# Low products eight places behind the high ones in the feed-forward stages of a two-layer hybrid block

## The chip, the cores and the metric

The kernel runs on one core of one Trainium2 chip. The metric is device time in microseconds (us). The kernel before takes 2301.96 us, the median of 3 runs (2301.77 to 2302.32).

## What is computed

Two layers, each a mixer (four kinds of attention, left out here) and a gated feed-forward part, on 256 positions of width 2048, in float32. The change touches only the up projection of the feed-forward part:

```python
def reference(x, norm_mix_pre, ...):
    ...
    for l in range(DEPTH):
        ...
        hin = _rms_norm(x, norm_mlp_pre[l])
        u = hin @ mlp_w_up[l]                    # 256x2048 @ 2048x11264
        u_pad = jnp.pad(u, ((0, 0), (CONV_WIDTH - 1, 0), (0, 0)))
        conv = mlp_conv_b[l] + mlp_conv_w[l][0] * u_pad[:, 0:s_len]
        for tap in range(1, CONV_WIDTH):
            conv = conv + mlp_conv_w[l][tap] * u_pad[:, tap:tap + s_len]
        gate, up = jnp.split(conv, 2, axis=-1)
        y = (jax.nn.gelu(gate, approximate=True) * up) @ mlp_w_down[l]
        x = x + _rms_norm(y, norm_mlp_post[l])
```

## The kernel before

**Split numbers.** TensorE takes a rounded float32 format here (float32r), so each float32 operand is used as a sum of a high and a low part. The activations lie in four tiles `HL0` to `HL3`, each 128 x 4 x 512: for each of the 16 slices `k` of the contraction, 256 columns of high parts and 256 of low parts. A weight tile is split on the chip: ScalarE (ACT) copies the loaded tile `raw` into `hi` (line 192), VectorE (DVE) subtracts to get `lo` (line 195). A **high product** multiplies a 128 x 128 piece of `hi` with all 512 columns of a slice; a **low product** multiplies the matching piece of `lo` with the 256 high columns alone. Both add into one PSUM bank.

**Units and granules.** One unit is 128 output columns of the up projection: 16 slices, so 16 high and 16 low products into one bank. Its weights come as two granules of 128 x 1024 (eight slices each). In each feed-forward stage 88 units run. The first three go through `start_block`, which also moves the activations into `HL0` to `HL3`; the other 85 are issued by `w_unit` (line 635), one unit after another. Then `out_units` (line 693) does the down projection with products of 512 columns.

**Order of the products.** `mm_runs` (line 426) issues the eight high products of a unit's first granule, then its eight low ones; for the second granule the low ones, then the high ones. Along the stage that makes runs of 16 low products (two half runs of one unit) and of 16 high products (the end of one unit and the start of the next):

```python
        for f in (los, his) if h else (his, los):
            f()
```

`start_block` uses `mm_w` (line 417) for its last pieces, in which low and high products alternate (lines 421 and 422).

**What sets the order elsewhere.** The program order of every engine is fixed when the program is built. `run_gran` (line 282) goes through one granule: `fill("v")` lets every waiting chain of small work take one step, `ready` (line 215) issues the loads and splits up to `LOOK` = 5 granules ahead, then come the products, `used` marks the granule's tiles as free for later ones (six `hi` and six `lo` tiles go round, line 204: the split of a granule may be issued only after the granule six before it was marked), and `fill("pe")`. When a unit's second granule is done, `launch` puts its evacuation among the chains (lines 1476 to 1506): ScalarE copies one half of the bank to `u`, VectorE adds the other, scales by the row norm `r2bc`, runs the three-tap convolution, and gate and up are joined in `y`. The scale `r2bc` is made near the start of each stage by the chain `rows` (line 488): GpSimd writes `diag`, one TensorE product (line 498) spreads it over the partitions, and ScalarE copies the result (line 500). There are eight PSUM banks, and `room` (line 279) advances chains until one is free.

Of the kernel before, what the change touches and what calls it, by code (L numbers as in the profile page):

```python
# [22 lines left out]
KT = D // 128  # L23
FF = 5632
NF = FF // 128
# [12 lines left out]
SPLIT_US = 1.15  # L38
# [97 lines left out]
def hybrid_kernel(ctx, tc, a):  # L136
    nc = tc.nc
    V, SC, TE, GP = nc.vector, nc.scalar, nc.tensor, nc.gpsimd
# [3 lines left out]
    ps = ctx.enter_context(tc.tile_pool(name="ps", bufs=1, space=bass.MemoryType.PSUM))  # L142
# [6 lines left out]
    def take(kind):  # L149
        live[kind] += 1  # L150
        assert live[kind] <= cap[kind], kind

    def drop(kind, n=1):
        live[kind] -= n
        assert live[kind] >= 0, kind

    def bank():
        take("ps")
        return ps.tile([128, 512], F32, tag="ps", name="bank", bufs=8)
# [4 lines left out]
    def gran(src, c0, n, whole=False):  # L164
        return Granule(src[:, c0:c0 + n], n, whole)

    def add(f, *gs):
        work.append((f, gs))
# [32 lines left out]
    def prep(upto, how=split):  # L201
        while state["gran"] <= min(upto, len(grans) - 1):
            i = state["gran"]
            if i >= HL_BUFS and grans[i - HL_BUFS].uses > 0:
                return
            g = grans[i]
            load(i + RAW_BUFS - 1)
            if state["load"] <= i:
                return
            if not g.whole:  # L210
                g.hi, g.lo = split_tiles()
                how(g, 0, g.n)
            state["gran"] += 1

    def ready(g, look=LOOK):
        prep(g.idx + look)
        assert g.idx < state["gran"]

    def used(g):
        g.uses -= 1  # L220
# [5 lines left out]
    def launch(gen, cost=0.0):  # L226
        c = Chain(gen)
        budget[0] -= cost
        if c.kind is not None:
            active.append(c)  # L230
        return c

    def may(c):
        return (all(live[k] + n <= lim[k] for k, n in c.need.items())
                and (c.cond is None or c.cond()))

    def step(c):
        c.step()
        if c.kind is None:
            active.remove(c)  # L240

    def fill(kind):
        n = 0
        for c in list(active):
            if c.kind == kind and may(c):
                step(c)
                n += 1
        return n

    def start(gain):  # L250
        budget[0] = min(budget[0] + gain, 2.0)
        n = 0
        while budget[0] > 0:
            for i in range(min(3, len(queue))):
                cost, fn, cond = queue[i]
                if cond is None or cond():
                    c = Chain(fn())
                    if not may(c):
                        continue
                    del queue[i]  # L260
                    budget[0] -= cost
                    active.append(c)
                    if c.kind == "pe":
                        step(c)
                    n += 1
                    break
            else:
                break
        return n
# [4 lines left out]
    def force(cond):  # L274
        while not cond():
            n = fill("v") + fill("pe") + start(1.0)
            assert n or budget[0] <= 0, "no chain can go on"

    def room(kind, n=1):
        force(lambda: live[kind] + n <= cap[kind])  # L280

    def run_gran(g, us, emit):
        fill("v")
        ready(g)
        emit()
        used(g)
        fill("pe")
        start(us - SPLIT_US)
# [25 lines left out]
    HL = [None] * 4  # L314
# [52 lines left out]
    def hview(k):  # L367
        return HL[k // 4][:, k % 4, :256]
# [57 lines left out]
    def mm_runs(o, g, h):  # L426
        def his():
            for k in range(8 * h, 8 * h + 8):
                TE.matmul(o, lhsT=g.hi[:, k % 8 * 128:k % 8 * 128 + 128], rhs=HL[k // 4][:, k % 4, :],  # L429
                          start=(k == 0), stop=(k == KT - 1))  # L430

        def los():
            for k in range(8 * h, 8 * h + 8):
                TE.matmul(o[:, :256], lhsT=g.lo[:, k % 8 * 128:k % 8 * 128 + 128], rhs=hview(k),  # L434
                          start=False, stop=False)

        for f in (los, his) if h else (his, los):
            f()
# [196 lines left out]
    def w_unit(src, evac, cost):  # L635
        u = src
        gs = [gran(u, 0, 1024), gran(u, 1024, 1024)]
        box = {}

        def part(h):  # L640
            def run():
                def emit():
                    if h == 0:
                        room("ps")
                        box["a"] = bank()
                    mm_runs(box["a"], gs[h], h)
                run_gran(gs[h], 2.56, emit)
                if h == 1:
                    launch(evac(box["a"]), cost)
            return run  # L650
        add(part(0), gs[0])
        add(part(1), gs[1])

    def x_units(srcs, width, evac, cost):
        box = {}
# [196 lines left out]
    def over():  # L852
        while ends:
            ends.pop()()
# [15 lines left out]
    def mixer(l):  # L870
# [542 lines left out]
        for h in range(4):  # L1413
            main.append(lambda h=h: w_unit(W[l, h], evac_nsa_q(h), 1.9))
# [45 lines left out]
    def mlp(l):  # L1460
        st = {}

        def begin():
            over()
            es = ExitStack()
            mp = es.enter_context(tc.tile_pool(name=f"mlp{l}", bufs=1, reuse_waits="tile"))
            st["es"], st["mp"], st["done"] = es, mp, set()
            st["cw"] = mp.tile([128, 2 * NF + 8, 4], F32, name="cw")[:, :2 * NF]
            GP.dma_start(out=st["cw"], in_=a["conv"][l])
            st["y"] = [mp.tile([128, 256], F32, name=f"y{j}") for j in range(NF)]  # L1470
            on_rows[0] = lambda: None

        def evac(i):
            j, up = divmod(i, 2)

            def f(p, first=None):
                yield "v", dict(u=1)
                mp = st["mp"]
                take("u")
                u = mp.tile([128, 256], F32, tag="u", name="u", bufs=4)  # L1480
                SC.activation(u, p[:, 256:], AF.Copy)  # L1481
                yield "v"
                V.tensor_tensor(u, u, p[:, :256], op=OP.add)  # L1483
                drop("ps")
                if first is not None:
                    add_first(u, first)
                if not scaled[0]:
                    yield "v", {}, is_scaled
                V.tensor_tensor(u, u, r2bc, op=OP.mult)  # L1489
                cv = mp.tile([128, 256], F32, tag="cv", name="cv", bufs=5)  # L1490
                w = st["cw"][:, i]
                V.tensor_scalar(cv, u, w[:, 2:3], w[:, 3:4], op0=OP.mult, op1=OP.add)  # L1492
                for tap in (1, 0):
                    n = 2 - tap
                    V.scalar_tensor_tensor(cv[:, n:], u[:, :256 - n], w[:, tap:tap + 1], cv[:, n:], op0=OP.mult,  # L1495
                                           op1=OP.add)
                drop("u")
                if not up:
                    yield "v"
                    g = mp.tile([128, 256], F32, tag="gl", name="gl", bufs=3)  # L1500
                    SC.activation(g, cv, AF.Gelu_apprx_tanh)  # L1501
                    st["g", j] = g
                else:
                    yield "v", {}, lambda: ("g", j) in st
                    V.tensor_tensor(st["y"][j], st["g", j], cv, op=OP.mult)
                    st["done"].add(j)
            return f

        UP = a["w_up"]
        start_block(2 * l + 1, [UP[l, i] for i in range(3)], [evac(i) for i in range(3)], mgs)  # L1510
        add(begin)
        for i in range(3, 2 * NF):
            w_unit(UP[l, i], evac(i), 0.0)
        out_units(2 * l + 1, lambda p_, k2: a["w_down"][l, p_, k2], NF, lambda k: st["y"][k],
                  lambda k: k in st["done"], mgs, tail_norm(mgs) if l < DEPTH - 1 else tail_out(mgs),
                  Left(lambda: st["mp"].tile([128, 256], F32R, tag="xs", name="xs", bufs=12), "xs"),
                  lambda: st["mp"].tile([128, 1024], F32, tag="gpost", name="gpost"), l == DEPTH - 1)

        def end():
            live["xs"] = 0  # L1520
            st["es"].close()
        add(lambda: ends.append(end))
# [3 lines left out]
    for l in range(DEPTH):  # L1526
        mixer(l)
        mlp(l)
# [95 lines left out]
```

## Time and profile before

| what | value |
|---|---|
| median of 3 runs | 2301.96 us |
| the profiled execution's own time | 2302.25 us |
| its span, from first to last instruction | 2300.5 us |
| mean granted TensorE clock | 0.999 of full speed |
| TensorE products (PE) | 2284.5 us busy, 99% of the span |
| weight loads (PEld) | 1971.7 us, 86% |
| VectorE | 1682.6 us, 73% |
| ScalarE | 1173.2 us, 51% |
| GpSimd | 50.0 us, 2% |
| DMA | 437.56 MB, mean 190 GB/s |

Busy times of products overlap, since an instruction's record runs from its start to a modelled end, while the next has started. So what one product costs is read here from start to start, in the timeline view: a row there gives the start in us, the time from the first start to the last end, engine, line, operation and tiles, the count of merged instructions, and in brackets the idle time before them and what ended it. A run of n products lasts from its row's start to the next row's start.

### The profile page before, as it was taken

What the parts mean: (1) busy time and instruction counts of PE and PEld (TensorE: products, weight loads), DVE (VectorE), ACT (ScalarE), POOL (GpSimd) and SP (SyncE); (2) the same over time, 40 slices, a digit from 0 to 9 for tenths busy, and PEclk for the clock granted to TensorE, in tenths of its full rate; (3) what the DMA queues carried; (4) which work ended last, traced back from release to release, by engine and by line L of the source; (5) the groups of instructions that cost most, each with busy time, mean ns of one, the idle gap of its engine ahead of it and who ended that gap; (6) DMA issues with size and microseconds to landing.
All of it is one profiled execution on the core that took longest, in us unless ns stands there. A gap on an engine that the chain in (4) does not pass through costs nothing.

```text
span 2300.5 us, 33209 instructions
## 1 busy us (share of the span) xinstructions
PE 2284.5 (99%) x12476; PEld 1971.7 (86%) x12476; DVE 1682.6 (73%) x2888; ACT 1173.2 (51%) x1915; POOL 50.0 (2%) x71
## 2 busy tenths in 40 slices
PE   8999999999999999999999999999999999999998
PEld 7888888888888888888888888888888888888887
DVE  6757656898888888565586576568988888885655
ACT  6454555644444444555464555556444444445543
POOL 1000000100000000000010000001000000000000
PEclk9999999999999999999999999999999999999999
DMA  8764455466556555656557645554665555556663
GB/s 277 249 218 150 159 167 199 156 207 199 192 184 192 190 187 184 202 187 211 176 189 239 209 141 174 174 193 158 207 197 188 191 190 185 191 191 194 202 194 116
DMA packets 122658, 437.56 MB, mean 190 GB/s; under 512 B 13888, under 2 KB 14016, under 8 KB 122496
## 3 DMA queue, kind: packets, MB, share of 16 engines
q1 hardware_dynamic: 120384, 429.40, 57.0%
q0 software_dynamic: 1824, 5.94, 0.9%
q8 instruction: 98, 1.61, 0.3%
q14 instruction: 64, 0.52, 0.1%
q10 hardware_dynamic: 288, 0.10, 0.0%
HBM read 433.28 MB, written 2.10 MB: 189 GB/s over the span
## 4 chain that ended last, share of the span: by engine, by line
PE 96%; ACT 1%; DVE 1%; issue 1%; DMA 0%; POOL 0%; SPq 0%; DVEq 0%; POOLq 0%; ACTq 0%
PE bank L429 36%; PE bank L434 19%; PE bank L728 9%; PE bank L726 9%; PE bank L727 9%; PE bank L678 2%; PE bank L680 2%; PE bank L679 2%; PE bank L1146 1%; PE bank L1068 1%; ACT hi L192 1%; PE bank L422 1%; PE bank L466 0%; PE bank L381 0%; DVE x L410 0%
## 5 line engine op out<-in xcount | busy, mean ns | idle before, releaser
L195 DVE TENSOR_TENSOR lo<-raw,hi 128x1024 fp32r<-128x1024 f32 (+1 forms) x786 | 948.3, 1211 | 499.1 <-ACT hi L192 498.3
L192 ACT ACTIVATE hi<-raw 128x1024 fp32r<-128x1024 f32 (+1 forms) x786 | 815.7, 1046 | 435.4 <-PE bank L728 265.5
L429 PE MATMUL bank<-HL,hi 128*128 128x512 f32 x3648 | 880.5, 392 | 0.4 <-DVE u L1483 0.4
L429 PEld LDWEIGHTS bank<-HL,hi 128*128 128x128 f32 x3648 | 669.3, 188 | 130.9 <-issue 2.8
L434 PEld LDWEIGHTS bank<-HL,lo 128*128 128x128 f32 x3648 | 469.5, 191 | 21.5 <-DVE qk L943 1.6
L434 PE MATMUL bank<-HL,lo 128*128 128x256 f32 x3648 | 480.3, 284 | 0.0
L726 PE MATMUL bank<-hi,xs 128*128 128x512 f32 x960 | 374.7, 390 | 0.0
L728 PE MATMUL bank<-hi,xs 128*128 128x512 f32 x960 | 373.9, 390 | 0.0
L727 PE MATMUL bank<-lo,xs 128*128 128x512 f32 x960 | 373.8, 389 | 0.0
L728 PEld LDWEIGHTS bank<-hi,xs 128*128 128x128 f32 x960 | 180.3, 188 | 37.4
L727 PEld LDWEIGHTS bank<-lo,xs 128*128 128x128 f32 x960 | 180.3, 188 | 37.3
L726 PEld LDWEIGHTS bank<-hi,xs 128*128 128x128 f32 x960 | 180.3, 188 | 36.7
L1495 DVE SCALAR_TENSOR_TENSOR cv<-u,cw,cv 128x255 f32<-128x255 f32 x352 | 170.1, 483 | 12.5
L1481 ACT ACTIVATE u<-bank 128x256 f32<-128x256 f32 x176 | 66.7, 381 | 202.2 <-PE bank L429 202.2
L1501 ACT ACTIVATE gl<-cv 128x256 f32<-128x256 f32 x88 | 36.8, 418 | 222.2 <-DVE cv L1495 222.2
L678 PE MATMUL bank<-hi,HL 128*128 128x512 f32 (+1 forms) x256 | 97.6, 381 | 0.5 <-ACT r2bc L500 0.5
L680 PE MATMUL bank<-hi,HL 128*128 128x512 f32 (+1 forms) x256 | 93.6, 366 | 0.0
L679 PE MATMUL bank<-lo,HL 128*128 128x512 f32 (+1 forms) x256 | 93.5, 365 | 0.0
L1489 DVE TENSOR_TENSOR u<-u,r2bc 128x256 f32<-128x256 f32 x176 | 74.9, 426 | 5.8
L1492 DVE TENSOR_SCALAR cv<-u,cw 128x256 f32<-128x256 f32 x176 | 72.7, 413 | 6.4
L1483 DVE TENSOR_TENSOR u<-u,bank 128x256 f32<-128x256 f32 x176 | 72.9, 414 | 0.0
L699 DVE TENSOR_TENSOR xs<-y,xs 128x256 fp32r<-128x256 f32 x176 | 72.2, 418 | 0.0
(212 smaller groups left out, 1388.5 us busy)
## 6 DMA issues: line engine op xcount, KB each, us to landing
raw<-in_w_up SPq DMA_DIRECT2D x352, 512.0 KB, 4.3
raw<-in_w_down SPq DMA_DIRECT2D x176, 512.0 KB, 3.7
raw<-in_w_cols SPq DMA_DIRECT2D x122, 512.0 KB, 4.2
raw<-in_w_out SPq DMA_DIRECT2D x64, 512.0 KB, 4.4
raw<-in_w_v SPq DMA_DIRECT2D x48, 512.0 KB, 4.3
raw<-in_cmp SPq DMA_DIRECT2D x32, 512.0 KB, 4.6
gpost<-in_gpost POOLq DMA_DIRECT2D x8, 512.0 KB, 7.2
raw<-in_w_x SPq DMA_DIRECT2D x8, 408.0 KB, 4.0
```

The source lines that it names most:

```text
L192: SC.activation(g.hi[:, c0:c0 + n], g.raw[:, c0:c0 + n], AF.Copy)
L195: eng.tensor_tensor(g.lo[:, c0:c0 + n], g.raw[:, c0:c0 + n], g.hi[:, c0:c0 + n].bitcast(F32), op=OP.subtract)
L429: TE.matmul(o, lhsT=g.hi[:, k % 8 * 128:k % 8 * 128 + 128], rhs=HL[k // 4][:, k % 4, :], start=(k == 0), stop=(k == KT - 1))
L434: TE.matmul(o[:, :256], lhsT=g.lo[:, k % 8 * 128:k % 8 * 128 + 128], rhs=hview(k), start=False, stop=False)
L678: TE.matmul(o, lhsT=h, rhs=wh, start=(K == 0), stop=False)
L679: TE.matmul(o, lhsT=h, rhs=wl, start=False, stop=False)
L680: TE.matmul(o, lhsT=lo, rhs=wh, start=False, stop=(K == KT - 1))
L726: TE.matmul(o, lhsT=h_, rhs=wh, start=(k[1] == 0), stop=False)
L727: TE.matmul(o, lhsT=h_, rhs=wl, start=False, stop=False)
L728: TE.matmul(o, lhsT=l_, rhs=wh, start=False, stop=(k[1] == nk - 1))
L1489: V.tensor_tensor(u, u, r2bc, op=OP.mult)
L1495: V.scalar_tensor_tensor(cv[:, n:], u[:, :256 - n], w[:, tap:tap + 1], cv[:, n:], op0=OP.mult, op1=OP.add)
```

## The change

`w_unit` is replaced, for the 85 later units of both feed-forward stages, by `w_lagged`. A granule's eight high products are issued at its own turn; its eight low products are issued in the next granule's turn, one ahead of each high product there. So the products alternate low, high, low, high from the second granule of the stage to the last, and a last step `flush` issues the eight low products that are left. The granule is marked as used, and a unit's evacuation launched, one granule later than before.

```diff
+    def w_lagged(units):
+        back = []
+
+        def lo(j):
+            g, h, o, _ = back[0]
+            k = 8 * h + j
+            TE.matmul(o[:, :256], lhsT=g.lo[:, j * 128:(j + 1) * 128], rhs=hview(k), start=False, stop=(k == KT - 1))
+
+        def done():
+            g, h, o, evac = back.pop()
+            used(g)
+            if h:
+                launch(evac(o))
+
+        def part(g, h, box, evac):
+            def run():
+                fill("v")
+                ready(g)
+                if h == 0:
+                    room("ps")
+                    box.append(bank())
+                for j in range(8):
+                    k = 8 * h + j
+                    if back:
+                        lo(j)
+                    TE.matmul(box[0], lhsT=g.hi[:, j * 128:(j + 1) * 128], rhs=HL[k // 4][:, k % 4, :],
+                              start=(k == 0), stop=False)
+                if back:
+                    done()
+                back.append((g, h, box[0], evac))
+                fill("pe")
+                start(2.56 - SPLIT_US)
+            return run
...
+        def flush():
+            for j in range(8):
+                lo(j)
+            done()
+        add(flush)
...
-        for i in range(3, 2 * NF):
-            w_unit(UP[l, i], evac(i), 0.0)
+        w_lagged([(UP[l, i], evac(i)) for i in range(3, 2 * NF)])
```

**TensorE, one unit in the middle of the first feed-forward stage.** The rows give line, operation, the bank written, the activation tile, the weight tile (`hi_4378` and `lo_4379` are the first granule, `hi_4384` and `lo_4385` the second), the moving columns, waits and count. Before:

```order
L429 MATMUL bank_4521<-HL0_4021,hi_4378 128x512 x3
L429 MATMUL bank_4521<-HL1_4022,hi_4378 128x512 x4
L434 MATMUL bank_4521<-HL0_4021,lo_4379 128x256 x4
L434 MATMUL bank_4521<-HL1_4022,lo_4379 128x256 x4
L434 MATMUL bank_4521<-HL2_4023,lo_4385 128x256 x4
L434 MATMUL bank_4521<-HL3_4024,lo_4385 128x256 x4
L429 MATMUL bank_4521<-HL2_4023,hi_4384 128x512 x4
L429 MATMUL bank_4521<-HL3_4024,hi_4384 128x512 x4
```

The same unit (now in `bank_4504`; line 679 is the high product, line 660 the low one) with the change, at the turn of its second granule:

```order
L660 MATMUL bank_4504<-HL0_4021,lo_4379 128x256
L679 MATMUL bank_4504<-HL2_4023,hi_4384 128x512
L660 MATMUL bank_4504<-HL0_4021,lo_4379 128x256
L679 MATMUL bank_4504<-HL2_4023,hi_4384 128x512
L660 MATMUL bank_4504<-HL0_4021,lo_4379 128x256
L679 MATMUL bank_4504<-HL2_4023,hi_4384 128x512
```

The runs of 16 are gone: each low product of the first granule stands ahead of a high product of the second.

**TensorE, the spreading product of line 498 near the start of the first feed-forward stage.** `bank_4388` is the first of the 85 units, `bank_4447` before and `bank_4431` now the second. Before:

```order
L434 MATMUL bank_4388<-HL3_4024,lo_4257 128x256 x4
L429 MATMUL bank_4388<-HL2_4023,hi_4256 128x512 [waits Activation_49]
L429 MATMUL bank_4388<-HL2_4023,hi_4256 128x512 x3
L429 MATMUL bank_4388<-HL3_4024,hi_4256 128x512 x4
L498 MATMUL bank_4436<-diag_73,cst_66 128x256 [waits PE_49,Pool_49]
L429 MATMUL bank_4447<-HL0_4021,hi_4262 128x512 [waits DVE_49,PE_49,Activation_49]
```

Now:

```order
L679 MATMUL bank_4388<-HL3_4024,hi_4256 128x512
L498 MATMUL bank_4422<-diag_73,cst_66 128x256 [waits PE_49,Pool_49]
L660 MATMUL bank_4388<-HL2_4023,lo_4257 128x256 [waits DVE_49]
L679 MATMUL bank_4431<-HL0_4021,hi_4262 128x512 [waits Activation_49]
L660 MATMUL bank_4388<-HL2_4023,lo_4257 128x256
L679 MATMUL bank_4431<-HL0_4021,hi_4262 128x512
```

Line 498 moved ahead by eight low products, one low product follows it, and the first high product of the next bank waits for ScalarE alone where it waited for VectorE too.

**TensorE, the end of the first feed-forward stage.** Line 726 before and line 772 now are the first product of the down projection. Before:

```order
L429 MATMUL bank_8990<-HL2_4023,hi_8877 128x512 [waits Activation_49]
L429 MATMUL bank_8990<-HL2_4023,hi_8877 128x512 x3
L429 MATMUL bank_8990<-HL3_4024,hi_8877 128x512 x4
L726 MATMUL bank_9043<-hi_8906,xs_9007 128x512 [waits PE_49,Activation_49]
L727 MATMUL bank_9043<-lo_8907,xs_9007 128x512 [waits DVE_49]
```

Now:

```order
L679 MATMUL bank_8973<-HL3_4024,hi_8886 128x512
L660 MATMUL bank_8973<-HL2_4023,lo_8887 128x256 [waits DVE_49]
L660 MATMUL bank_8973<-HL2_4023,lo_8887 128x256 x3
L660 MATMUL bank_8973<-HL3_4024,lo_8887 128x256 x4
L772 MATMUL bank_9031<-hi_8914,xs_9015 128x512 [waits PE_49,Activation_49]
L773 MATMUL bank_9031<-lo_8915,xs_9015 128x512 [waits DVE_49]
```

The stage ends on a run of eight low products where it ended on eight high ones. The order of DMA issues and of GpSimd's instructions is the same before and now.

## Rows read from the trace of the kernel before

**Rows 1.** The page: busy time of TensorE, and the chain that ended last.
```profile
PE 2284.5 (99%) x12476; PEld 1971.7 (86%) x12476; DVE 1682.6 (73%) x2888; ACT 1173.2 (51%) x1915; POOL 50.0 (2%) x71
...
PE 96%; ACT 1%; DVE 1%; issue 1%; DMA 0%; POOL 0%; SPq 0%; DVEq 0%; POOLq 0%; ACTq 0%
```
**Rows 2.** Window, first feed-forward stage: length; PE, PEld, DVE, ACT, POOL busy; clock; DMA.
```profile
443.00:911.00 468.00, 467.80 (x2689) 413.46 (x2689) 400.51 (x654) 218.21 (x299) 0.00 (x0) 1.00 0.60 193
```
**Rows 3.** Timeline of TensorE, first feed-forward stage: first, middle and last runs.
```profile
445.32 2.08 PE L434 MATMUL bank<-HL,lo 128*128 128x256 f32 x16
...
645.72 2.08 PE L434 MATMUL bank<-HL,lo 128*128 128x256 f32 x16
647.63 3.82 PE L429 MATMUL bank<-HL,hi 128*128 128x512 f32 x16
651.28 2.08 PE L434 MATMUL bank<-HL,lo 128*128 128x256 f32 x16
...
907.35 2.08 PE L434 MATMUL bank<-HL,lo 128*128 128x256 f32 x16
...
911.10 0.39 PE L726 MATMUL bank<-hi,xs 128*128 128x512 f32 x1
```
**Rows 4.** Timeline of TensorE in a down projection: products of 512 columns only.
```profile
1002.68 0.39 PE L728 MATMUL bank<-hi,xs 128*128 128x512 f32 x1
...
1024.44 0.39 PE L728 MATMUL bank<-hi,xs 128*128 128x512 f32 x1
```
**Rows 5.** Timeline of TensorE, alternating products of the second feed-forward stage's start block.
```profile
1574.76 0.27 PE L421 MATMUL bank<-HL,lo 128*128 128x256 f32 x1
...
1578.92 0.27 PE L421 MATMUL bank<-HL,lo 128*128 128x256 f32 x1
1579.03 0.40 PE L422 MATMUL bank<-HL,hi 128*128 128x512 f32 x1
1579.26 1.98 PE L429 MATMUL bank<-HL,hi 128*128 128x512 f32 x8
1581.08 2.08 PE L434 MATMUL bank<-HL,lo 128*128 128x256 f32 x16
```
**Rows 6.** The same for the first feed-forward stage's start block.
```profile
431.95 0.40 PE L422 MATMUL bank<-HL,hi 128*128 128x512 f32 x1
...
436.81 0.40 PE L422 MATMUL bank<-HL,hi 128*128 128x512 f32 x1
```
**Rows 7.** Timeline of TensorE, alternating products at the start of the kernel.
```profile
22.08 1.03 PE L381 MATMUL bank<-cst,x 128*128 128x128 f32 x8
22.87 0.36 PE L421 MATMUL bank<-HL,lo 128*128 128x256 f32 x1
...
23.30 0.28 PE L421 MATMUL bank<-HL,lo 128*128 128x256 f32 x1
...
29.66 0.28 PE L421 MATMUL bank<-HL,lo 128*128 128x256 f32 x1
```
**Rows 8.** Timeline of TensorE, GpSimd, ScalarE and VectorE around line 498, first feed-forward stage.
```profile
437.04 1.98 PE L429 MATMUL bank<-HL,hi 128*128 128x512 f32 x8
...
442.62 0.60 PE L498 MATMUL bank<-diag,cst 128*128 128x256 f32 x2
443.42 0.47 PE L429 MATMUL bank<-HL,hi 128*128 128x512 f32 x1 [0.20 <-DVE u L1483]
...
438.98 1.99 POOL L493 TENSOR_SCALAR diag<-cst,r 128x128 f32<-128x128 f32 x2
...
443.25 0.38 ACT L500 ACTIVATE r2bc<-bank 128x256 f32<-128x256 f32 x1 [0.95 <-PE bank L498]
...
442.87 0.41 DVE L1483 TENSOR_TENSOR u<-u,bank 128x256 f32<-128x256 f32 x1
```
**Rows 9.** Timeline of VectorE and ScalarE before the first feed-forward stage ends.
```profile
905.74 0.38 ACT L1481 ACTIVATE u<-bank 128x256 f32<-128x256 f32 x1 [2.65 <-PE bank L429]
...
908.25 0.75 DVE L699 TENSOR_TENSOR xs<-y,xs 128x256 fp32r<-128x256 f32 x2
```

More of the change, by code (lines that the diff above doesn't have):

```diff
@@ L652, in w_unit @@
         add(part(1), gs[1])
+    def w_lagged(units):
[28 more added lines that the diff above has]
+            return run
+        for src, evac in units:
+            box = []
+            for h in range(2):
+                g = gran(src, h * 1024, 1024)
+                add(part(g, h, box, evac), g)
+        def flush():
[3 more added lines that the diff above has]
+        add(flush)
     def x_units(srcs, width, evac, cost):
```

## The prediction

> **What bounds the kernel now.** The page comes first: TensorE is busy 99% of the span, and 96% of the chain that ended last is TensorE [rows 1]. So the time is the sum of the steps from the start of one product to the start of the next, and another engine matters only where it makes TensorE wait. The window over the first feed-forward stage says the same of the place that is changed (the second one reads alike): the clock is granted in full (1.00, the 2.4 GHz level), TensorE is busy throughout, VectorE for 400.5 of 468 us, DMA engines for 0.60 of the time [rows 2]. There the question is only what a high and a low product cost in each order, and that is read in the timeline from row to row.
>
> Today's order: a run of 16 low products lasts 647.63 - 645.72 = 1.91 us, 0.119 each; the 16 high ones behind it last 651.28 - 647.63 = 3.65 us, 0.228 each; a unit takes 5.57 us [rows 3]. More exactly, from the first full low run to the last lie 83 units: (907.35 - 445.32) / 83 = 5.567 us [rows 3]. That is **0.3479 us for a pair** of one high and one low product.
>
> What an unbroken row of high products costs is seen in the down projection: 96 products in 1024.44 - 1002.68 = 21.76 us, 0.2267 each [rows 4]. Sixteen of these would be 3.627 us, and the high run takes 3.65: the first products behind a low run are some 0.02 us slow in sum. It is this **price of the turn from low to high** that alternation could remove, once a unit, or else charge at every pair.
>
> **What alternation costs.** The kernel already alternates in its start blocks, and the trace shows two speeds.
> - Fast: from 1574.76 to 1578.92 lie 12 pairs, 4.16 us, 0.3467 us a pair [rows 5]. The high run behind it takes 1581.08 - 1579.26 = 1.82 us for eight, 0.2275 each: no debt is left over [rows 5]. The start block of the first stage, counted with its beginning, gives (436.81 - 431.95) / 14 = 0.3471 [rows 6].
> - Slow: from 23.30 to 29.66 us lie 18 pairs, 6.36 us, 0.3533 us a pair, with no recovery to the end [rows 7].
>
> What comes before differs. The slow stretch begins with a low product that had been waiting behind eight transposes, and alternates strictly from there [rows 7]. The fast ones begin with a high product, and `mm_w` puts two low and two high products side by side where a granule begins (line 424). Which of these makes the speed, the trace does not tell.
>
> In the changed kernel the 85 units alternate from the second granule on, in one go but for the product of line 498. Behind that, today, the first high product waits, and the run of eight then lasts 445.32 - 443.42 = 1.90 us [rows 3, 8], that is 0.31 for the one that waited and seven at 0.227: no debt. The changed order has a high product waiting at the same place, so I take the fast speed, 0.3469 (between the 0.3467 of [rows 5] and the 0.3471 of [rows 6]).
>
> **The sum, part by part.**
> - *Pairs.* 85 units x 16 pairs x 2 stages = 2720 pairs. 2720 x (0.3479 - 0.3469) = **2.7 us less**. The bounds are the two stretches: 2720 x (0.3479 - 0.3467) = 3.3 us less, and 2720 x (0.3533 - 0.3479) = 14.7 us more.
> - *Line 498.* It comes 0.96 us earlier (eight low products at 0.12). Eight high products (1.82 us) and eight pairs (2.78 us) from 437.04 put it at 441.64; `diag` is ready at 438.98 + 1.99 = 440.97 [rows 8], so it does not wait. But the bank of the next high product is now the one that line 498 wrote: with all eight in use, the only one that comes free without VectorE is freed by ScalarE's copy of line 500, and the order shows a wait for ScalarE alone. Today the copy starts 0.03 us after line 498 ends at 443.22 and takes 0.38; the next product starts 0.14 us behind the VectorE row that frees its bank (442.87 + 0.41 = 443.28, start 443.42) [rows 8]. Shifted: line 498 ends at 442.24, the copy at 442.65, the high product starts at 442.79. The one low product in between covers 0.12 us. So TensorE idles about 0.43 us where it now idles 0.20 [rows 8]: 0.23 us more, twice: **0.5 us more**.
> - *End of the stage.* A low run of eight now stands ahead of the down projection, so one turn from low to high remains per stage: 0.02 us, twice. The first left operands of the down projection (lines 698, 699) are issued later relative to the end: today VectorE finishes them 3.3 us after the unit's evacuation starts on ScalarE (908.25 + 0.75 - 905.74) [rows 9], with the down projection at 911.10 [rows 3]. Now that evacuation starts with the last granule's turn, 3.7 us before the down projection; it leaves 0.3 to 0.4 us, and the product that needs the VectorE part is third in line. **Nothing**, but thin: without that cover it costs what it is late, a few tenths.
> - *Splits and banks.* A granule is marked one turn later, so splits are issued four granules ahead, not five. Four granules are 4 x 2.78 = 11.1 us, and the split itself is two operations of about 1.1 us each. A low tile is also needed one granule later than its high tile. VectorE does the same work (86% busy [rows 2]) in the same order but for the first units. Nothing; if splits did come late, TensorE would stop for each.
> - *Evacuation.* One granule later, 2.8 us, in the cover of the next unit; one more bank is held. Nothing but for the stage's start, above. DMA issues keep their order.
>
> Together -2.7 + 0.5 = -2.2 to -2.3 us. The profiled execution takes 2302.25 us (span 2300.5), so 2300.0 us for one like it; it stood 0.29 us above the median of 2301.96, so the median becomes **2299.7 us**. That is 0.1% faster; a measurement of this kernel tells about 0.2% (4.6 us) from no change, so the forecast is a small gain that counts as the same.
>
> **Rivals.**
> 1. *The slow alternation holds* (the other side). After line 498 the products alternate strictly behind a wait, as in the slow stretches, and neither a pair nor a granule's waits brought those back [rows 7]. Price: 14.7 + 0.5 = 15 us, **2317 us**; if only one stage falls into it, 7.3 - 1.4 + 0.5 = 6.4 us, 2308. It decides from a pair of 0.3477 us up (2720 x 0.0002 no longer covers the 0.5), and can be measured from 0.3494. For it: the 18 pairs did not recover. Against it: the two start blocks [rows 5, 6] and the clean run behind line 498. Both stages 0.09, one stage 0.05.
> 2. *The order has no price.* The extra 0.02 us behind a low run would come from something else at that point (VectorE and ScalarE turn to the new unit then) and stays. Then only the wait at line 498 is new: **2302.4 us**. Against it: behind alternating products the high run is clean [rows 5]. Chance 0.07. The Trainium skill, "TensorE: Matmul & The Clock Gate", Back-to-back issue gap, is on this side: isolated matmuls step at columns / 2.4 + 2.5 ns, which is 216 ns for 512 columns and 109 for 256 in whatever order. The trace differs: 226.7 ns [rows 4] and 119 [rows 3].
> 3. *The low product gets cheaper.* Half the columns of a high product at half its step is 0.113 us, and single low products in the alternating stretch do show 0.11 (1578.92 to 1579.03) [rows 5]. If the high one kept 0.2267, a pair would be 0.340: 2720 x 0.0079 = 21.5 us less, **2281 us**. Against it: the high products between them stretch to 0.23 (1579.03 to 1579.26) [rows 5]. Chance 0.04.
> 4. *Splits come late.* One granule of lead less, with VectorE at 86%, lets TensorE wait in the units behind the stage's start, where VectorE has three evacuations to catch up. At one wait of about 1 us in every eighth unit, 20 us: 2320 us. Against it: 11 us of lead. Chance 0.03.
>
> **How the numbers follow.** The forecast has 0.72, with its own range 2298.3 to 2301.5. The range 2297.0 to 2308.5 takes in the forecast, rival 2 and the one-stage half of rival 1, 0.84 less the forecast's own tails, so some 0.8; it leaves out both stages slow, the cheaper low product and late splits. Faster by over 0.2% (below 2297.4): rival 3 and the forecast's low tail, 0.07. Slower by over 0.2% (above 2306.6): rival 1 and rival 4, 0.17. Same: 0.76.
>
> **What would show it.** In the timeline of the changed kernel's feed-forward stage, lines 660 and 679 alternate without idle time, and two successive first low products of a unit stand 5.55 us apart (5.567 today). If rival 1 holds, they stand 5.65 us apart; if rival 2, 5.57; if rival 3, 5.44. Line 498 starts about 1 us earlier, and the high product two rows behind it shows an idle time of about 0.4 us ended by ScalarE's line 500. The down projection's first products show no idle time; VectorE's line 745 ends before them. The prediction is wrong if TensorE shows waits for line 192 or 195, or if the spacing drifts within the stage.

## The result, and the profile after

The changed kernel takes **2316.87 us**, the median of 5 runs (2316.28 to 2317.76), against 2301.96 us for the kernel before in the same five rounds (2301.74 to 2302.78): a ratio of 1.0065, 95% interval 1.0054 to 1.0075. It is 14.9 us slower where a gain of 2.3 us was forecast, outside the range, and at the time of rival 1 (2317 us).

The page of the changed kernel: busy times, the chain that ended last, and the two groups of products in question (line 679 high, line 660 low; group rows give count, busy us, mean ns of one, idle us before them and what ended it).

```profile
PE 2298.2 (99%) x12476; PEld 1967.5 (85%) x12476; DVE 1682.6 (73%) x2888; ACT 1158.8 (50%) x1915; POOL 50.2 (2%) x71
...
PE 97%; DVE 1%; ACT 1%; issue 0%; POOL 0%; DMA 0%; SPq 0%; DVEq 0%; POOLq 0%; ACTq 0%
...
L679 PE MATMUL bank<-HL,hi 128*128 128x512 f32 x2720 | 959.6, 399 | 0.7 <-ACT r2bc L500 0.7
L660 PE MATMUL bank<-HL,lo 128*128 128x256 f32 x2720 | 762.0, 281 | 0.0
```

Against [rows 1], TensorE is busy 13.7 us longer, with the same count of products, and 97% of the chain is still TensorE. The 2720 pairs of the two stages waited 0.7 us in all, for ScalarE's line 500 and for nothing else. So no other engine took the time: TensorE works through the same products more slowly. The window over the first feed-forward stage, with the columns of [rows 2], shuts out the clock:

```profile
443.00:917.00 474.00, 474.00 (x2686) 411.11 (x2685) 397.79 (x648) 209.51 (x297) 0.00 (x0) 1.00 0.59 189
```

The clock is granted in full, the DMA share and VectorE's work are as they were in [rows 2], and TensorE is never idle. The timeline of TensorE then says where the time lies: first product of the stage, its first pairs, line 498, the first pairs behind it, the end of the stage, and the first product of the down projection (line 772); then the same two ends for the second stage.

```profile
436.06 1.98 PE L679 MATMUL bank<-HL,hi 128*128 128x512 f32 x8
437.87 0.28 PE L660 MATMUL bank<-HL,lo 128*128 128x256 f32 x1
...
440.34 0.28 PE L660 MATMUL bank<-HL,lo 128*128 128x256 f32 x1
440.46 0.39 PE L679 MATMUL bank<-HL,hi 128*128 128x512 f32 x1
440.69 0.59 PE L498 MATMUL bank<-diag,cst 128*128 128x256 f32 x2
440.93 0.47 PE L660 MATMUL bank<-HL,lo 128*128 128x256 f32 x1
441.75 0.50 PE L679 MATMUL bank<-HL,hi 128*128 128x512 f32 x1 [0.36 <-ACT r2bc L500]
442.09 0.28 PE L660 MATMUL bank<-HL,lo 128*128 128x256 f32 x1
...
916.62 1.12 PE L660 MATMUL bank<-HL,lo 128*128 128x256 f32 x8
917.57 0.40 PE L772 MATMUL bank<-hi,xs 128*128 128x512 f32 x1
...
1585.82 1.98 PE L679 MATMUL bank<-HL,hi 128*128 128x512 f32 x8
...
2067.34 0.40 PE L772 MATMUL bank<-hi,xs 128*128 128x512 f32 x1
```

- *The stage.* From its first product to the down projection it lasts 917.57 - 436.06 = 481.51 us; before, 911.10 - 437.04 = 474.06 [rows 3, 8]. That is 7.45 us more. The second stage now lasts 2067.34 - 1585.82 = 481.52 us, where it took 2053.33 - 1579.26 = 474.07 before, so the two stages give 14.9 us, the whole difference of the medians. The two profiled executions differ by only 14.0 us in their spans (2314.5 against 2300.5); the changed kernel's reached the first stage 0.98 us earlier, ahead of every changed product.
- *The pairs.* Between the low product at 442.09 and the first of the eight that end the stage lie 1343 pairs: (916.62 - 442.09) / 1343 = **0.35333 us a pair**, the slow speed of [rows 7] to the last digit that can be read.
- *From the start.* Between 437.87 and 440.34 lie seven pairs, 0.3529 each: the slow alternation is there before line 498, right behind a row of eight high products at full pace, with no wait in front of it.

Between single starts, which the trace keeps to the nanosecond and the timeline shows rounded to 10, the slow alternation is a cycle of three pairs: low 117 ns, high 241; low 120, high 236; low 113, high 233; 1060 in all. These are called its first, second and third pair below. The fast one of the start blocks [rows 5] is a cycle of two pairs: low 118, high 231; low 112, high 232; 693 in all, 346.7 a pair.

### The profile page after: what moved, and what is told of

Same layout as the page of the kernel before. It is cut to its first block, busy times and chain, and to the rows that moved or that the text cites. A ratio compares the mean times of both kernels' runs of the same rounds, so it can differ in the third digit from the quotient of the medians.

```text
span 2314.5 us, 33207 instructions
## 1 busy us (share of the span) xinstructions
PE 2298.2 (99%) x12476; PEld 1967.5 (85%) x12476; DVE 1682.6 (73%) x2888; ACT 1158.8 (50%) x1915; POOL 50.2 (2%) x71
## 4 chain that ended last, share of the span: by engine, by line
PE 97%; DVE 1%; ACT 1%; issue 0%; POOL 0%; DMA 0%; SPq 0%; DVEq 0%; POOLq 0%; ACTq 0%
PE bank L679 28%; PE bank L660 14%; PE bank L772 9%; PE bank L774 9%; PE bank L773 9%; PE bank L429 9%; PE bank L434 5%; PE bank L724 2%; PE bank L726 2%; PE bank L725 2%; PE bank L422 1%; PE bank L1192 1%; PE bank L1114 1%; PE bank L421 0%; PE bank L466 0%
## 5 line engine op out<-in xcount | busy, mean ns | idle before, releaser
L192 ACT ACTIVATE hi<-raw 128x1024 fp32r<-128x1024 f32 (+1 forms) x786 | 799.8, 1045 | 360.4 <-PE bank L774 265.4
L679 PE MATMUL bank<-HL,hi 128*128 128x512 f32 x2720 | 959.6, 399 | 0.7 <-ACT r2bc L500 0.7
L660 PE MATMUL bank<-HL,lo 128*128 128x256 f32 x2720 | 762.0, 281 | 0.0
L679 PEld LDWEIGHTS bank<-HL,hi 128*128 128x128 f32 x2720 | 511.1, 188 | 128.6 <-ACT r2bc L500 1.3
L660 PEld LDWEIGHTS bank<-HL,lo 128*128 128x128 f32 x2720 | 513.0, 189 | 0.2
L429 PE MATMUL bank<-HL,hi 128*128 128x512 f32 x928 | 230.7, 395 | 0.0
L429 PEld LDWEIGHTS bank<-HL,hi 128*128 128x128 f32 x928 | 169.1, 188 | 33.6 <-issue 1.6
L434 PEld LDWEIGHTS bank<-HL,lo 128*128 128x128 f32 x928 | 120.7, 190 | 8.3 <-DVE qk L989 1.6
L434 PE MATMUL bank<-HL,lo 128*128 128x256 f32 x928 | 127.4, 285 | 0.0
```

The source lines that it names most:

```text
L192: SC.activation(g.hi[:, c0:c0 + n], g.raw[:, c0:c0 + n], AF.Copy)
L660: TE.matmul(o[:, :256], lhsT=g.lo[:, j * 128:(j + 1) * 128], rhs=hview(k), start=False, stop=(k == KT - 1))
L679: TE.matmul(box[0], lhsT=g.hi[:, j * 128:(j + 1) * 128], rhs=HL[k // 4][:, k % 4, :], start=(k == 0), stop=False)
```

## The experiments

In the experiments the high product is line 677 and the low one line 660, unless said otherwise; "H" and "l" stand for them in the strings that set the order. "A double" is a place where two high products and two low products stand side by side in an otherwise strict alternation. The first question was what chooses the speed. Theory A: strictness; a double, as `mm_w` has one at each granule, brings the fast speed, and it then holds. Theory B: the lag; a low product in another granule, slice and bank than its neighbour makes the pair slow.

**One double in each stage.** In the changed kernel, the fifth granule's eight places are taken from a string; in the first stage they begin high, low, low, high (`first` is "HllH"), in the second low, low, high, high ("llHH").

```diff
-                for j in range(8):
+                def high(j):
...
-                    if back:
-                        lo(j)
...
+                n[0] += 1
+                seq = "lHlHlHlHlHlHlHlH" if back else "HHHHHHHH"
+                if n[0] == 5:
+                    seq = first + seq[4:]
+                at = dict(l=0, H=0)
+                for c in seq:
+                    (lo if c == "l" else high)(at[c])
+                    at[c] += 1
```

> The changed kernel with one spot per stage reordered, in the fifth granule: high low low high in the first stage, low low high high in the second; all else alternates strictly. Theory A (strict alternation has two speeds that hold themselves, and two low products side by side set the fast one): the pair goes from 0.3533 us to 0.347 behind the spot and stays there to the end of the stage; some 2690 pairs x 0.0063 = 17 us less than the changed kernel, about 2300 us. If only one of the two orders switches it, 2308. Theory B (a pair is slow because its low product uses another granule, another activation slice and every second time another bank than its high product): 0.3533 throughout, 2317 us.

Measured: 2316.78 us (2316.34 to 2317.64), ratio 1.0064, interval 1.0049 to 1.0079. The timeline around the double and at the stage's end, first stage, then second:

```profile
448.58 0.62 PE L677 MATMUL bank<-HL,hi 128*128 128x512 f32 x2
449.05 0.40 PE L660 MATMUL bank<-HL,lo 128*128 128x256 f32 x2
449.28 0.40 PE L677 MATMUL bank<-HL,hi 128*128 128x512 f32 x1
449.51 0.28 PE L660 MATMUL bank<-HL,lo 128*128 128x256 f32 x1
...
918.03 1.12 PE L660 MATMUL bank<-HL,lo 128*128 128x256 f32 x8
...
1598.78 0.63 PE L677 MATMUL bank<-HL,hi 128*128 128x512 f32 x2
1599.24 0.28 PE L660 MATMUL bank<-HL,lo 128*128 128x256 f32 x1
...
2067.75 1.12 PE L660 MATMUL bank<-HL,lo 128*128 128x256 f32 x8
```

Behind it lie 1326 pairs at (918.03 - 449.51) / 1326 = 0.3533, and in the second stage, with the other order, 1326 at (2067.75 - 1599.24) / 1326 = 0.3533. A double does not bring the fast speed, or not these two: theory A fell in this form.

**A double at the start of every granule.** The same code with one string for all granules (the lines taken out are those of the run above):

```diff
-                seq = "lHlHlHlHlHlHlHlH" if back else "HHHHHHHH"
-                if n[0] == 5:
-                    seq = first + seq[4:]
+                seq = "HllHlHlHlHlHlHlH" if back else "HHHHHHHH"
```

> The changed kernel with high low low high at the start of every granule, so that two highs and two lows stand side by side once in eight pairs, as in the start blocks. Theory A: the fast speed, with a price for each spot; four products around such a spot in the start block took some 0.01 to 0.015 us more than two fast pairs, so 340 x 0.0125 = 4 us above strict fast alternation: 2302 to 2305 us. Theory B: 2317 us or more.

Measured: 2307.07 us (2306.53 to 2307.68), ratio 1.0022, interval 1.0013 to 1.0031: between the two speeds. The timeline shows how; three doubles in a row (each row of two highs and the row of two lows behind it):

```profile
497.86 0.63 PE L677 MATMUL bank<-HL,hi 128*128 128x512 f32 x2
498.33 0.40 PE L660 MATMUL bank<-HL,lo 128*128 128x256 f32 x2
...
500.68 0.63 PE L677 MATMUL bank<-HL,hi 128*128 128x512 f32 x2
501.15 0.39 PE L660 MATMUL bank<-HL,lo 128*128 128x256 f32 x2
...
503.46 0.62 PE L677 MATMUL bank<-HL,hi 128*128 128x512 f32 x2
```

One granule of eight pairs lasts 500.68 - 497.86 = 2.82 us, the next 503.46 - 500.68 = 2.78, and so on in turn: every other granule is fast. Each double changes the speed. In the single starts, each change to fast leaves the slow cycle behind its third pair; the doubles that had failed in the run before stood behind a second pair, in both stages. That made the next theory (C, below).

**No lag, strict alternation.** The kernel before, whose 85 units now issue high, low, high, low with both products of a slice side by side in one bank (lines 443 and 444 of that kernel):

```diff
+    def mm_pairs(o, g, h):
+        for k in range(8 * h, 8 * h + 8):
+            w = slice(k % 8 * 128, k % 8 * 128 + 128)
+            TE.matmul(o, lhsT=g.hi[:, w], rhs=HL[k // 4][:, k % 4, :], start=(k == 0), stop=False)
+            TE.matmul(o[:, :256], lhsT=g.lo[:, w], rhs=hview(k), start=False, stop=(k == KT - 1))
...
-                    mm_runs(box["a"], gs[h], h)
+                    mms(box["a"], gs[h], h)
...
-            w_unit(UP[l, i], evac(i), 0.0)
+            w_unit(UP[l, i], evac(i), 0.0, mm_pairs)
```

> The kernel before with strict alternation inside each granule: high product, then the low product of the same slice, same granule, same bank, no lag. It is entered from the start block's fast alternation over two highs side by side, with no double low. Theory A: the entry sets the slow speed or the line 498 product does, 0.3533 a pair, about 2317 us. Theory B: 0.347 a pair, about 2300 us.

Measured: 2316.16 us (2316.01 to 2317.01), ratio 1.0062, interval 1.0047 to 1.0077. The timeline at the seam between the start block and the first unit, and at the first and last low product behind the product of line 498:

```profile
436.15 0.40 PE L422 MATMUL bank<-HL,hi 128*128 128x512 f32 x1
436.38 0.39 PE L443 MATMUL bank<-HL,hi 128*128 128x512 f32 x1
436.61 0.28 PE L444 MATMUL bank<-HL,lo 128*128 128x256 f32 x1
...
443.06 0.28 PE L444 MATMUL bank<-HL,lo 128*128 128x256 f32 x1
...
917.58 0.28 PE L444 MATMUL bank<-HL,lo 128*128 128x256 f32 x1
```

(917.58 - 443.06) / 1343 = 0.3533. Without the lag, the other bank and the other slice the alternation is as slow as with them: theory B fell. And the seam is telling: the start block before it runs fast, two high products meet there (436.15 and 436.38), and the alternation behind them is slow at once.

**Runs of eight.** To learn whether the price of a turn was rightly read, the kernel before with eight high products, then eight low ones, in every granule. So a unit has two turns from low to high, not one.

```diff
-                          start=(k == 0), stop=(k == KT - 1))
+                          start=(k == 0), stop=(k == KT - 1 and not eight))
...
-                          start=False, stop=False)
+                          start=False, stop=(eight and k == KT - 1))
...
-        for f in (los, his) if h else (his, los):
+        for f in (los, his) if h and not eight else (his, los):
```

> The kernel before with eight highs and eight lows in every granule, so twice as many turns from low to high in the 85 units, 170 more in all. If a turn costs the same 0.02 us whatever the run behind it, 170 x 0.02 = 3.4 us more: 2305.4 us. If the price grows with the length of the low run, about 2302 us.

Measured: 2305.45 us (2305.02 to 2306.16), ratio 1.0015, interval 1.0005 to 1.0025. The timeline in the middle of a stage:

```profile
600.33 2.00 PE L429 MATMUL bank<-HL,hi 128*128 128x512 f32 x8
602.17 1.11 PE L434 MATMUL bank<-HL,lo 128*128 128x256 f32 x8
603.12 2.00 PE L429 MATMUL bank<-HL,hi 128*128 128x512 f32 x8
```

Eight high products take 1.84 us, eight of the unbroken row [rows 4] 8 x 0.2267 = 1.81: again some 0.02 to 0.03 us a turn. Against 2302.03 us for the kernel before in these rounds, 170 more turns cost 3.4 us, 0.020 each. The price is real and is the same for runs of eight and sixteen: the gain that the change was to take was there, 170 turns x 0.020 = 3.4 us in the two stages.

**One double, one pair later.** Theory C: there are two steady alternations, each holds itself, and when two equal products meet, the place in the cycle decides which one follows. Its rival D: the place in the program decides, since in the run with a double in each granule first and second halves of a unit also alternate.

```diff
                 if n[0] == 5:
-                    seq = first + seq[4:]
+                    seq = "lHHllHlHlHlHlHlH"
```

> The kernel with the change, with one double in the fifth granule of each stage, as in the run with one double, but one pair later: low, high, high, low, low, high, and so on, so that the clean cycle of three pairs is left right behind its third pair (low 113, high 233 ns). Theory C (two steady alternations, 346.7 and 353.3 ns a pair; each holds itself until two equal products meet, and which one follows depends on the pair of the cycle behind which they meet): fast from there to the end of each stage, 1343 pairs x 6.6 ns = 8.9 us less per stage, 2316.8 - 17.7 = 2299.1 us. Theory D (what counts is the place: doubles in granules that are the second half of a unit make the alternation fast, doubles in first halves make it slow, as every other granule was fast in the run with a double in each): the fifth granule is a first half, so slow throughout, 2316.8 us.

Measured: **2299.55 us** (2298.63 to 2300.01, 11 runs), against 2301.89 us for the kernel before (21 runs): ratio 0.9989, interval 0.9980 to 0.9998. The timeline of the first stage, around the double and at the end:

```profile
448.52 0.28 PE L660 MATMUL bank<-HL,lo 128*128 128x256 f32 x1
448.64 0.63 PE L677 MATMUL bank<-HL,hi 128*128 128x512 f32 x2
449.11 0.39 PE L660 MATMUL bank<-HL,lo 128*128 128x256 f32 x2
449.33 0.40 PE L677 MATMUL bank<-HL,hi 128*128 128x512 f32 x1
449.57 0.28 PE L660 MATMUL bank<-HL,lo 128*128 128x256 f32 x1
...
908.90 1.10 PE L660 MATMUL bank<-HL,lo 128*128 128x256 f32 x8
```

(908.90 - 449.57) / 1325 = 0.34667 us a pair, to the end of the stage, and in the second stage the same. One low product moved behind one high product in each stage saves 17.3 us (2316.87 - 2299.55). With the next run it is the quickest version here, below both kernels, though below the kernel before by 0.1% only, within the 0.2% of the forecast's bound.

**The double in later granules.** The edit of the first experiment, high, low, low, high at the start of a granule, only in the seventh granule of the first stage and the sixth of the second (`turn` is 7 and 6):

```diff
-                if n[0] == 5:
+                if n[0] == turn:
-                    seq = first + seq[4:]
+                    seq = "HllH" + seq[4:]
```

> The same edit as in the run with one double (high, low, low, high at the start of one granule), only in another granule: the seventh in stage 1, the sixth in stage 2. By the cycle of three pairs the seventh granule starts behind the third pair (low 113, high 233) and the sixth behind the first (low 117, high 241), where the fifth started behind the second (low 120, high 236). Theory C: fast from the seventh granule of stage 1, 1327 x 6.6 ns = 8.8 us less; in stage 2 a double behind the first pair has not been seen yet: slow to the end gives 2308.0 us in all, fast 2299.2. Theory D: the seventh granule is a first half (slow), the sixth a second half (fast): 2308.0 us too, but with the stages exchanged, which the two stages' lengths tell.

Measured: 2299.76 us (2298.55 to 2300.38, 10 runs), ratio 0.9989, interval 0.9980 to 0.9999. The timeline around the double and at the end, first stage, then second:

```profile
453.93 0.63 PE L677 MATMUL bank<-HL,hi 128*128 128x512 f32 x2
...
454.86 0.28 PE L660 MATMUL bank<-HL,lo 128*128 128x256 f32 x1
...
908.99 1.11 PE L660 MATMUL bank<-HL,lo 128*128 128x256 f32 x8
...
1592.06 0.64 PE L677 MATMUL bank<-HL,hi 128*128 128x512 f32 x2
...
1593.00 0.28 PE L660 MATMUL bank<-HL,lo 128*128 128x256 f32 x1
...
2049.91 1.11 PE L660 MATMUL bank<-HL,lo 128*128 128x256 f32 x8
```

Both stages are fast: (908.99 - 454.86) / 1310 = 0.34667 and (2049.91 - 1593.00) / 1318 = 0.34667. The seventh granule is a first half, like the fifth, where the same edit did nothing; so D fell. The double of the second stage stood behind a first pair (117, 240), which C had left open: it brings the fast speed too. Only behind a second pair (120, 236) did a double leave the slow cycle as it was.

The start blocks, whose doubles no run moved, bear this out at other places of the program. In the nine traces they hold 36 doubles with at least three pairs on either side. 15 of them stand behind a first pair, and fast pairs follow all 15. Another 15 stand behind a pair of low 117, high 230 (347 ns, so already fast), and all of these stay fast. Two stand behind a second pair, at 13.25 us in the changed kernel and at 13.58 in the run without lag, and the pairs behind both are slow. The other four, all near 14 us, follow a pair that belongs to none of these.

**A second double in the fast alternation.** The double one pair later, and another in the 31st granule: 208 pairs behind it in the first stage (`again` is "lHHllHlHlHlHlHlH"), 207 in the second ("HllHlHlHlHlHlHlH").

```diff
                 if n[0] == 5:
                     seq = "lHHllHlHlHlHlHlH"
+                if n[0] == 31:
+                    seq = again
```

> The kernel with one double in the fifth granule one pair later (2299.55 us), plus a second double in the 31st granule of each stage: in stage 1 again one pair behind the granule's start, 208 pairs behind the first double, in stage 2 at the granule's start, 207 pairs behind it. In the run with a double in every granule, 8 pairs apart, every double met in the fast alternation ended it. Theory C with the cycle of two pairs as the phase: an even distance of 208 leaves the fast cycle behind the same pair (low 112, high 233) as those did and ends it, 1112 pairs x 6.67 ns = 7.4 us more; an odd distance leaves it behind the other pair (low 118, high 231), which has not been seen: if that keeps it, 2299.55 + 7.4 = 2307.0 us; if every double ends the fast alternation, 2314.4 us. A rival, that an alternation once fast for long stays so whatever meets it: 2299.6 us.

Measured: 2314.16 us (2313.76 to 2314.80), ratio 1.0053, interval 1.0036 to 1.0070. The timeline around the second double and at the end, first stage, then second:

```profile
520.42 0.63 PE L677 MATMUL bank<-HL,hi 128*128 128x512 f32 x2
...
521.35 0.28 PE L660 MATMUL bank<-HL,lo 128*128 128x256 f32 x1
...
916.03 1.12 PE L660 MATMUL bank<-HL,lo 128*128 128x256 f32 x8
...
1668.42 0.62 PE L677 MATMUL bank<-HL,hi 128*128 128x512 f32 x2
...
1669.35 0.28 PE L660 MATMUL bank<-HL,lo 128*128 128x256 f32 x1
...
2064.38 1.11 PE L660 MATMUL bank<-HL,lo 128*128 128x256 f32 x8
```

(916.03 - 521.35) / 1117 = 0.3533: the fast alternation had held for 208 pairs and ended at the second double. In the second stage the double stands behind the other pair (118, 230), and (2064.38 - 1669.35) / 1118 = 0.3533 again. So a double behind either pair of the fast cycle ends it, the case with 2314.4 us; a fast alternation isn't kept by having lasted.

One thing did not go as laid out: in the first stage of this execution the first double stood behind a first pair (117, 241), not behind a third as in the run with the same order up to there, since behind the wait at line 498 the cycle had begun one pair further on. It brought the fast speed all the same. So the order of the products does not fix the pair behind which a place is met; here both pairs that were met lead to the fast speed.

## Why the prediction was wrong

**Pairs: the step that failed.** "The changed order has a high product waiting at the same place, so I take the fast speed, 0.3469." The term came out as 2720 x (0.35333 - 0.3479) = 14.8 us more, not 2.7 us less. The text had two stretches for the same thing and no row that told which condition made the speed; it then took a clean run of high products behind line 498 as a sign that a wait clears the way. That run has no low products in it, so it could say nothing of how an alternation goes on. The changed trace refutes the sign twice: the pairs are slow behind eight clean high products, before any wait, and slow again behind the wait at line 498. The 18 slow pairs without recovery [rows 7] told rightly that an alternation keeps the speed that it has. That was the argument for rival 1, and its 14.7 us were the right price.

**What no row could tell.** Which speed the new stretch would take could not be read from the trace before, not from [rows 7] either. The same products in the same order, behind the same transposes, run fast at the start of the changed kernel, where nothing was changed:

```profile
23.39 0.28 PE L421 MATMUL bank<-HL,lo 128*128 128x256 f32 x1
...
28.59 0.28 PE L421 MATMUL bank<-HL,lo 128*128 128x256 f32 x1
```

That is (28.59 - 23.39) / 15 = 0.3467 us a pair, where [rows 7] have 0.3533. Of the nine traces three are slow there (the kernel before, the run with one double in each stage and the run with one double one pair later) and six fast. So the order alone does not choose the speed there, and what differs at the entry of that stretch stays open. The changed stage, by contrast, came out slow each time: behind the eight high products and again behind line 498, in both stages, in all five traces that have this order up to the first double.

**What the fast speed would have given.** 2299.7 us were forecast for it; the run with one double one pair later, fast for all but the first granules, took 2299.55. With the pairs at 0.34667 us and line 498 as measured (below) the same sum gives 2298.9. So the other terms and the sum were sound to some 0.6 us, and the error is that one choice.

**The price of the turn** was read rightly: 0.02 us, shown by the runs of eight. Rival 2, by which the order has no price, fell. The Trainium skill, "TensorE: Matmul & The Clock Gate", Back-to-back issue gap, gives isolated matmuls a step that depends on their columns alone. The traces disagree: a pair of the same two products took 0.3479 us in runs of sixteen and 0.3467 or 0.3533 in alternation. Rival 3 fell as well: single low products did get down to 112 ns, but the high ones beside them took 230 to 241, not 227, and no order here brought a pair below 0.3467 over a long stretch.

**Line 498.** Its place was right: 440.69 - 436.06 = 4.63 us into the stage, where 441.64 - 437.04 = 4.60 was forecast. TensorE's idle time behind it is 0.36 us and ends with ScalarE's line 500; 0.43 was forecast, and 0.20 stood there before [rows 8]. So it costs 0.16 us a stage rather than 0.23.

**End of the stage, splits and banks, evacuation.** Nothing was forecast and nothing shows: the first products of the down projection follow without idle time, no pair waits for line 192 or 195, and the pairs keep their spacing to the end. Rival 4 fell.

**The sum.** 14.8 for the pairs and 0.3 for line 498 make 15.1 us; measured are 14.9.

## What to carry to other kernels

Where long and short products alternated on TensorE here without a pause, the cost of a pair was a state that held itself, not a sum of two prices: a short stretch of the trace gives the price only of that state, and if two stretches disagree, the spread is the forecast until a run tells what chooses. One irregularity set the state for hundreds of microseconds, so try the same order shifted by one or two products before giving it up, and look in the trace for what a wait ahead of it does to the cycle. Runs of sixteen equal products cost only 0.001 us a pair more than the best alternation, and each of the units measured in the kernel before took between 5.565 and 5.568 us, so no second speed shows in them.

## What was not expected of the hardware

- Two steady speeds of one strict alternation of products of 256 and 512 columns at the full clock: a cycle of three pairs in 1060 ns (353.3 a pair) and one of two pairs in 693 ns (346.7). Each held for as long as it was left alone, over 1300 pairs. At the start of the kernel the fast speed also shows as an even row of low 117, high 230.
- Two high and then two low products change slow to fast behind the first or third pair of the slow cycle, leave it slow behind the second, and change fast to slow behind either pair of the fast cycle. Two low and then two high were tried once, behind a second pair, and left it slow.
- The same program order, 20 pairs at the start of the kernel, ran slow in three traces and fast in six.
- What inside TensorE makes the two cycles stays open: weight loads, the moving data and the writes to the bank were not separated. Nor is it settled what sets the cycle, and the place in it, at the start of an alternation and behind a wait.
